# Eleven instead of five dense products between two groups of chunk-local products

## The chip, the cores and the metric

The kernel runs on one core of a Trainium2 chip. The metric is the device time of one execution in microseconds. The engines of the core are TensorE (PE, with its weight loads as PEld), VectorE (DVE), ScalarE (ACT), GpSimd (POOL) and SyncE (SP), which issues most loads. Each works through its own queue in order, and semaphores hold an instruction until what it needs is done.

## What is computed

One encoder block on 512 tokens of width 2048, in float32: a recurrent branch and an attention branch share one normalised input; each is gated and projected, and the two are merged, projected and normalised.

```python
h = rms_norm(x, norm_g)
proj = jnp.einsum('btd,de->bte', h, w_in)             # 2048 -> 86 strips of 128
shifted = centred_shift(proj[..., :SHIFT_WIDTH], shift_mu)
...
def _wkv_step(S, inp):                                # 512 steps, 16 heads of 64, both directions
    w, kk, b, k, v, r = inp
    sa = jnp.einsum('dbhvk,dbhk->dbhv', S, -kk)
    S = S * w[..., None, :] + sa[..., None] * b[..., None, :] + v[..., :, None] * k[..., None, :]
    o = jnp.einsum('dbhvk,dbhk->dbhv', S, r)
    return S, o
...
o_r = rwkv7_bidir(...) * jax.nn.silu(z_r)
o_a = axial_gqa(q, k, v, q_norm_g, k_norm_g) * jax.nn.silu(z_a)     # 16 heads, 4 key heads
p_r = jnp.einsum('btc,cd->btd', o_r, w_branch_rwkv)
p_a = jnp.einsum('btc,cd->btd', o_a, w_branch_attn)
merged = jax.nn.sigmoid(g_r) * p_r + jax.nn.sigmoid(g_a) * p_a
return rms_norm(x + jnp.einsum('btd,de->bte', merged, w_out), final_norm_g)
```

## The kernel before, in words

**Dense products.** Activations stand transposed, 16 tiles of 128 features by 512 tokens, each split into a high part `hh` and a low part `hl` (float32r). A strip is 128 output features; its weights come in quarters of four 128x128 blocks: SP loads `raw`, ScalarE casts it to `wh` (line 264), VectorE subtracts to get `wl` (line 265; in the attention stage every other quarter on GpSimd). Three products a block (line 291) accumulate a strip in `acc`, a PSUM tile of 128x512 of which there are two. Twelve products make a quarter. All dense products that the program weaves are on line 291: 84 whole strips and two early ones of the input projection, then 16 strips `share_r` on `oq` (the recurrent branch's output) and 16 strips `share_a` on `oah`, `oal` (the output of attention); 4932 in all.

**Weaving.** `Weave.run` writes TensorE's order out. Everything that is not a dense product is a task, a generator that issues some instructions and then yields three numbers: the time in ns that TensorE is thought to need for what was issued (`cost`), the time to wait before the task goes on (`wait`), and a flag that it needs. While no task is due, one dense product after another is issued, each counted as 217 ns. So a `wait` of 1000 puts five dense products behind a step. Dense products are a fixed stock: what is issued at one place is missing at a later one. In the recurrent stage TensorE's order is exactly this one. From the attention stage on, the tile framework's scheduler reorders it somewhat, and it sets the order of the other engines' queues throughout.

**Stages.** First the input's normalisation and transposition. Then the recurrent stage: eight tiles of two heads, both directions, 512 tokens in eight chunks of 64. For tile i `stage_a(i)` prepares the decays, `tile_task(i)` computes, `stage_e(i)` normalises the result (reductions on lines 722 to 730, transpositions `pg` on line 736, gating on lines 742 and 743). Meanwhile the strips of the input projection run; those that are only needed later are stored by ScalarE's queue (line 476). Then the attention stage: 64 units, each scores (`sc`, lines 882 and 883), a maximum, an exponential (line 888), a scaling on GpSimd (line 891), transpositions (`pT`, line 899), a split into `ph` and `pl`, and for each two units the output product (`po`, line 914); beside them the rest of the input projection, then `share_r`, whose gates GpSimd loads (`tgm`, line 956). Then `share_a`, then the output projection.

**The place of the change.** `tile_task` begins with the products inside the chunks (`lr`, line 571), in four groups of two chunks. A group is eight products into two PSUM tiles `lr[0]` and `lr[1]`, taken in turn; in the trace each is two records, so a group is 16. PSUM tiles of this kind (`g_tile`) number three. ScalarE copies a part out (lines 573 and 576), VectorE multiplies the rest with masks (lines 574, 575, 577, 578). Behind the last group come `pv`, `tb` and `pcf`, then 230 dense products while VectorE inverts small blocks, then `pq`, `px` and the serial chain over the chunks (`pa`, `pu`, `px2`). The yield that is changed stands at the end of each of the four groups:

```python
        ac.copy(LB[hi_, :, two, :], lr[1][hi_, :, :, C:128])
        ve.tensor_tensor(out=AL[lo_, :, two, 1, :], in0=lr[1][lo_], in1=m2(lo_, 1, 0, 128), op=ALU.mult)
        ve.tensor_tensor(out=L2[hi_, :, two, 1, 0:C], in0=lr[1][hi_, :, :, 0:C], in1=m2(hi_, 1, 0, C), op=ALU.mult)
        yield 1720, 1000, None
```

Of the kernel before, what the change touches and what calls it, by code (L numbers as in the profile page):

```python
# [224 lines left out]
def emit_all(nc, tc, A, out, dbg):  # L225
# [194 lines left out]
    def g_tile(nm):  # L420
        return pr_.tile([128, T], F32, tag="g", name=nm, bufs=3)
# [124 lines left out]
    def tile_task(i):  # L546
# [16 lines left out]
        for c in range(0, NC, 2):  # L563
            two = slice(c, c + 2)

            lr = [g_tile("lr").rearrange("p (d c t) -> p d c t", d=2, c=2) for _ in range(2)]
            for d in range(2):
                for j in range(2):
                    for eo in range(2):
                        h0 = 64 * eo  # L570
                        pe.matmul(lr[eo][:, d, j, :], lhsT=BK[h0:h0 + 64, d, c + j, :], rhs=AL[h0:h0 + 64, d, c + j, eo, :], start=True, stop=True)  # L571
            m2 = lambda rows, eo, c0_, c1_: mk[rows, :, eo, c0_:c1_].unsqueeze(2).to_broadcast([64, 2, 2, c1_ - c0_])
            ac.copy(LB[lo_, :, two, :], lr[0][lo_, :, :, 0:C])
            ve.tensor_tensor(out=AL[hi_, :, two, 0, :], in0=lr[0][hi_], in1=m2(hi_, 0, 0, 128), op=ALU.mult)
            ve.tensor_tensor(out=L2[lo_, :, two, 0, C:128], in0=lr[0][lo_, :, :, C:128], in1=m2(lo_, 0, C, 128), op=ALU.mult)
            ac.copy(LB[hi_, :, two, :], lr[1][hi_, :, :, C:128])
            ve.tensor_tensor(out=AL[lo_, :, two, 1, :], in0=lr[1][lo_], in1=m2(lo_, 1, 0, 128), op=ALU.mult)
            ve.tensor_tensor(out=L2[hi_, :, two, 1, 0:C], in0=lr[1][hi_, :, :, 0:C], in1=m2(hi_, 1, 0, C), op=ALU.mult)
            yield 1720, 1000, None
        pv = g_tile("pv")  # L580
        for j in range(4):
            pe.transpose(pv[:, j * 128:(j + 1) * 128], v[:, j * 128:(j + 1) * 128], ident)
# [172 lines left out]
    for i in range(NT):  # L755
        W.add(3, stage_a(i))
        W.add(0, tile_task(i))
# [334 lines left out]
```

## Time and profile before

| what | value |
|---|---|
| median of three runs | 1799.01 us (1795.56 to 1801.14) |
| the profiled execution | 1803.82 us, of which the span of the trace is 1801.7 us |
| TensorE, matmuls | 1724.6 us busy, 96% |
| VectorE | 1215.6 us, 67% |
| ScalarE | 814.0 us, 45% |
| GpSimd | 564.4 us, 31% |
| chain that ended last | PE 42%, DVE 3%, all others 1% or less |

The span is one execution as the hardware profiler recorded it. Matmuls are pipelined, and the ends of their records are modelled, so "busy" is the time in which some matmul was under way, and not a measure of how well it ran. The granted clock is the share of TensorE's full speed that the chip granted in a stretch: 1.00 is 2.4 GHz, 0.50 is 1.2 GHz.

### The profile page before, as it was taken

What the parts mean: (1) busy time and instruction counts of PE and PEld (TensorE: products, weight loads), DVE (VectorE), ACT (ScalarE), POOL (GpSimd) and SP (SyncE); (2) the same over time, 40 slices, a digit from 0 to 9 for tenths busy, and PEclk for the clock granted to TensorE, in tenths of its full rate; (3) what the DMA queues carried; (4) which work ended last, traced back from release to release, by engine and by line L of the source; (5) the groups of instructions that cost most, each with busy time, mean ns of one, the idle gap of its engine ahead of it and who ended that gap; (6) DMA issues with size and microseconds to landing.
All of it is one profiled execution on the core that took longest, in us unless ns stands there. A gap on an engine that the chain in (4) does not pass through costs nothing. (4 is left out here: it accounts for less than half of the span.)

```text
span 1801.7 us, 26028 instructions
## 1 busy us (share of the span) xinstructions
PE 1724.6 (96%) x8972; PEld 1440.6 (80%) x8972; DVE 1215.6 (67%) x2354; ACT 814.0 (45%) x1827; POOL 564.4 (31%) x830
## 2 busy tenths in 40 slices
PE   7999999998999998999998999999999999999997
PEld 6877887887887886887887887888788888888876
DVE  6577849759849949858859949543868876443342
ACT  5544444444444444354354453444567665332231
POOL 3131242152152233053152241033546553331110
PEclk9999999999999999999999999999999999999999
DMA  6564323323323322423323323325424332435452
GB/s 219 172 198 118 84 69 103 96 59 101 101 60 101 96 66 86 114 65 96 103 65 104 96 71 94 106 77 161 120 83 137 110 94 80 151 113 152 131 164 111
DMA packets 96851, 194.87 MB, mean 108 GB/s; under 512 B 11088, under 2 KB 11344, under 8 KB 95312
## 3 DMA queue, kind: packets, MB, share of 16 engines
q1 hardware_dynamic: 77616, 152.18, 29.5%
q10 hardware_dynamic: 15264, 28.46, 4.4%
q0 software_dynamic: 3840, 12.59, 2.3%
q8 instruction: 71, 1.16, 0.3%
q14 instruction: 60, 0.49, 0.1%
HBM read 162.77 MB, written 30.41 MB: 107 GB/s over the span
## 5 line engine op out<-in xcount | busy, mean ns | idle before, releaser
L291 PE MATMUL acc<-hh,wl 128*128 128x512 f32 (+1 forms) x1388 | 554.0, 399 | 5.3 <-DVE wl L265 5.2
L291 PE MATMUL acc<-hh,wh 128*128 128x512 f32 (+1 forms) x1388 | 556.5, 401 | 0.6 <-ACT wh L264 0.2
L291 PE MATMUL acc<-hl,wh 128*128 128x512 f32 (+1 forms) x1388 | 555.1, 400 | 1.6 <-DVE hl L386 1.2
L264 ACT CAST wh<-raw 128x512 fp32r<-128x512 f32 x472 | 292.3, 620 | 507.4 <-PE acc L291 347.6
L265 DVE TENSOR_TENSOR wl<-raw,wh 128x512 fp32r<-128x512 f32 x439 | 327.4, 748 | 284.4 <-ACT wh L264 275.8
L291 PEld LDWEIGHTS acc<-hh,wl 128*128 128x128 f32 x1388 | 264.3, 190 | 57.4 <-DVE wl L265 8.5
L291 PEld LDWEIGHTS acc<-hl,wh 128*128 128x128 f32 x1388 | 265.1, 191 | 51.9 <-DVE hl L386 3.1
L291 PEld LDWEIGHTS acc<-hh,wh 128*128 128x128 f32 x1388 | 265.2, 191 | 51.3 <-ACT wh L264 1.4
L673 POOL TENSOR_SCALAR SV<-VT 64x128 f32<-64x128 f32 x256 | 81.2, 317 | 208.3 <-PE px L700 116.5
L706 DVE SCALAR_TENSOR_TENSOR SV<-px,PC,sd 64x64 f32<-64x64 f32 x224 | 63.5, 283 | 81.2 <-PE px L700 75.3
L689 POOL TENSOR_SCALAR sd<-SV,PC 64x64 f32<-64x64 f32 x224 | 89.5, 400 | 17.4
L608 DVE TENSOR_TENSOR B<-B,tm 128x30 f32<-128x30 f32 (+14 forms) x240 | 82.2, 342 | 6.0
L607 DVE TENSOR_TENSOR tm<-B 128x30 f32<-128x30 f32 (+14 forms) x240 | 82.2, 343 | 5.8
L291 PE MATMUL acc<-oq,wh 128*128 128x512 f32 x256 | 83.4, 396 | 1.9 <-ACT oq L946 1.9
L1023 PE MATMUL of<-wl,mh 128*128 128x512 f32 x192 | 75.1, 391 | 2.2 <-DVE wl L265 2.2
L527 POOL TENSOR_TENSOR ks<-ks,k 128x512 f32<-128x512 f32 x8 | 15.8, 1969 | 192.0 <-ACT wh L264 111.7
L571 PE MATMUL lr<-AL,BK 64*128 64x128 f32 x512 | 49.9, 314 | 26.6 <-DVE s L728 13.7
L678 PEld LDWEIGHTS pa<-SV,AL 128*128 128x128 f32 x512 | 68.0, 193 | 8.7 <-POOL SV L673 2.3
L1024 PE MATMUL of<-wh,ml 128*128 128x512 f32 x192 | 74.7, 389 | 0.0
L700 PEld LDWEIGHTS px<-SV,L 128*128 128x128 f32 x512 | 68.6, 195 | 7.3 <-ACT SV L694 1.7
L571 PEld LDWEIGHTS lr<-AL,BK 64*128 64x128 f32 x512 | 41.2, 212 | 41.6 <-issue 14.2
L678 PE MATMUL pa<-SV,AL 128*128 128x64 f32 x512 | 67.3, 273 | 2.5 <-DVE SV L706 2.5
(688 smaller groups left out, 2938.8 us busy)
## 6 DMA issues: line engine op xcount, KB each, us to landing
raw<-in_w_in_dram SPq DMA_DIRECT2D x344, 256.0 KB, 3.1
raw<-in_wo_dram SPq DMA_DIRECT2D x64, 256.0 KB, 2.8
fsp<-tg ACTq DMA_DIRECT2D x60, 256.0 KB, 2.5
tsp<-la ACTq DMA_DIRECT2D x32, 256.0 KB, 3.6
la<-tsp SPq DMA_DIRECT2D x8, 1024.0 KB, 5.5
raw<-in_wbr_dram SPq DMA_DIRECT2D x32, 256.0 KB, 2.9
tgm<-fsp POOLq DMA_DIRECT2D x32, 256.0 KB, 3.6
raw<-in_wba_dram SPq DMA_DIRECT2D x32, 256.0 KB, 2.9
```

The costliest lines, as they stand in the source:

```text
L264: ac.copy(dst_hi, src)
L265: (eng or ve).tensor_tensor(out=dst_lo, in0=src, in1=f(dst_hi), op=ALU.subtract)
L291: pe.matmul(acc[:, tok], lhsT=w[1 if u == 2 else 0][:, j, :], rhs=(xl if u == 1 else xh)[:, kt, tok], start=(kt == 0 and u == 0 and tok.st ...
L571: pe.matmul(lr[eo][:, d, j, :], lhsT=BK[h0:h0 + 64, d, c + j, :], rhs=AL[h0:h0 + 64, d, c + j, eo, :], start=True, stop=True)
L607: se.tensor_tensor(out=tv, in0=B[:, 0:s, s:s + 1].to_broadcast([128, s, n]), in1=B[:, s:s + 1, s + 1:32].to_broadcast([128, s, n]), op=ALU ...
L608: se.tensor_tensor(out=B[:, 0:s, s + 1:32], in0=B[:, 0:s, s + 1:32], in1=tv, op=ALU.add)
L673: po.tensor_scalar(out=SV[v0:v0 + 64, d, eo], in0=src.unsqueeze(1).to_broadcast([64, 2, C]), scalar1=1.0, scalar2=0.0, op0=ALU.mult, op1=A ...
L678: pe.matmul(pa[:, d, eo, :], lhsT=AL[:, d, cc[d], eo, :], rhs=SV[:, d, eo, 0, :], start=True, stop=True)
L689: po.tensor_scalar(out=sd[h, d, eo, :], in0=SV[h, d, eo, 0, :], scalar1=PC[h, d, cc[d]:cc[d] + 1], scalar2=0.0, op0=ALU.mult, op1=ALU.add)
L700: pe.matmul(px2[:, d, eo, :], lhsT=L2[:, d, cc[d], eo, :], rhs=SV[:, d, eo, 1, :], start=True, stop=True)
L1023: pe.matmul(acc, lhsT=mh[:, dt, tok(tt)], rhs=w[1], start=False, stop=False)
L1024: pe.matmul(acc, lhsT=ml[:, dt, tok(tt)], rhs=w[0], start=False, stop=(dt == NKT - 1))
```

## The change

Two numbers of one yield: the time counted for a group falls from 1720 to 900 ns, the wait behind it rises from 1000 to 2300 ns. In the count of 217 ns a product that is eleven dense products instead of five. Nothing is computed otherwise.

```diff
--- before.py
+++ after.py
@@ -576,7 +576,7 @@
             ac.copy(LB[hi_, :, two, :], lr[1][hi_, :, :, C:128])
             ve.tensor_tensor(out=AL[lo_, :, two, 1, :], in0=lr[1][lo_], in1=m2(lo_, 1, 0, 128), op=ALU.mult)
             ve.tensor_tensor(out=L2[hi_, :, two, 1, 0:C], in0=lr[1][hi_, :, :, 0:C], in1=m2(hi_, 1, 0, C), op=ALU.mult)
-            yield 1720, 1000, None
+            yield 900, 2300, None
         pv = g_tile("pv")
         for j in range(4):
             pe.transpose(pv[:, j * 128:(j + 1) * 128], v[:, j * 128:(j + 1) * 128], ident)
```

What the planner makes of it is seen in the order of TensorE's queue. Below is what stands in tile 2 from the third group on, before (an `acc` row is one dense product, the `lr` row a whole group, `pg` belongs to the previous tile):

```order
L571 MATMUL lr<-AL,BK 128x128 x8
L291 MATMUL acc<-hh,wl 128x512
L291 MATMUL acc<-hh,wh 128x512
L291 MATMUL acc<-hl,wh 128x512
L291 MATMUL acc<-hh,wl 128x512
L291 MATMUL acc<-hh,wh 128x512
L571 MATMUL lr<-AL,BK 128x128 x8
L736 MATMUL pg<-con,ow 64x128 x8
L291 MATMUL acc<-hl,wh 128x512
L582 MATMUL pv<-con,v 128x128 x4
L633 MATMUL tb<-con,BK 128x128 x4
```

And now, from the same third group:

```order
L571 MATMUL lr<-AL,BK 128x128 x8
L291 MATMUL acc<-hh,wl 128x512
L291 MATMUL acc<-hh,wh 128x512
L291 MATMUL acc<-hl,wh 128x512
L291 MATMUL acc<-hh,wl 128x512
L291 MATMUL acc<-hh,wh 128x512
L291 MATMUL acc<-hl,wh 128x512
L291 MATMUL acc<-hh,wl 128x512
L736 MATMUL pg<-con,ow 64x128 x8
L571 MATMUL lr<-AL,BK 128x128 x8
L291 MATMUL acc<-hh,wh 128x512
L291 MATMUL acc<-hl,wh 128x512
```

Behind the third group there are seven dense products, then `pg`, then the fourth group; eleven dense products, of which two are shown, follow before `pv`. The first two gaps have eleven dense products each instead of five. A tile takes 426 dense products instead of 402 (in the first tile the third gap has eleven, too).

Since a strip is 48 products, the strips now end at other places of a tile, and ScalarE's queue changes with them. Before, its rows in tile 1 around the copies from `pq` (line 649) and from `px` (line 657) are these; line 476 is the store of a gate strip, whose data VectorE writes:

```order
L264 CAST wh<-raw 128x512
L473 ACTIVATE tg<-acc 128x512
L649 COPY LQ<-pq 32x8x32 x4
L476 DMA fsp<-tg 128x512
L657 COPY XP<-px 32x8x32 x4
L680 COPY a0s<-pa 64x128
```

Now:

```order
L649 COPY LQ<-pq 32x8x32 x4
L530 ACTIVATE e_2099<-cs_2093 128x512
L532 ACTIVATE la<-la 128x512
L531 ACTIVATE cs_2093<-cs_2093 128x512
L657 COPY XP<-px 32x8x32 x4
L680 COPY a0s<-pa 64x128
```

The store and its activation have gone from this place, and three exponentials of the next tile's decays (lines 530 to 532) stand there.

The dense products that the recurrent stage now takes are missing at the end of the attention stage. Before, TensorE's rows around the last output product `po` were these; `oq` rows belong to `share_r`, `oah` and `oal` rows to `share_a`:

```order
L291 MATMUL acc<-oq,wh 128x512 x2
L291 MATMUL acc<-oq,wl 128x512
L914 MATMUL po<-ph,VS 128x256 x4
L914 MATMUL po<-pl,VS 128x256 x4
L291 MATMUL acc<-oq,wh 128x512 x2
L291 MATMUL acc<-oq,wl 128x512
L291 MATMUL acc<-oah,wh 128x512
L291 MATMUL acc<-oal,wh 128x512
L291 MATMUL acc<-oah,wl 128x512
L291 MATMUL acc<-oah,wh 128x512
```

Now the last twelve rows up to the last `po` hold no dense product:

```order
L882 MATMUL sc<-KH,Q 128x512
L883 MATMUL sc<-KL,Q 128x512
L899 MATMUL pT<-con,pr 128x128 x4
L914 MATMUL po<-ph,VS 128x256 x4
L899 MATMUL pT<-con,pr 128x128 x4
L914 MATMUL po<-pl,VS 128x256 x4
L899 MATMUL pT<-con,pr 128x128 x4
L914 MATMUL po<-ph,VS 128x256 x4
L899 MATMUL pT<-con,pr 128x128 x4
L914 MATMUL po<-pl,VS 128x256 x4
L914 MATMUL po<-ph,VS 128x256 x4
L914 MATMUL po<-pl,VS 128x256 x4
```

Behind it stand six products of the first two `share_a` strips, which need the last head's output, and then the third strip. From the scores of unit 55 (counted from 1) to the last `po` there are twelve dense products, all of `share_a`.

## Rows read from the trace of the kernel before

**Rows 1.** the page, busy us (share of the span) and instructions of the engines

```profile
PE 1724.6 (96%) x8972; PEld 1440.6 (80%) x8972; DVE 1215.6 (67%) x2354; ACT 814.0 (45%) x1827; POOL 564.4 (31%) x830
```

**Rows 2.** who waited for it: us in total, times, longest us; TensorE

```profile
PE lr L571 <- DVE s L728: 13.7, 3, 5.0
PE lr L571 <- DVE L L575: 12.9, 6, 3.4
```

**Rows 3.** timeline of TensorE at `lr`: start us, us, tile, count [idle before <-releaser]

```profile
149.98 1.13 PE L571 MATMUL lr<-AL,BK 64*128 64x128 f32 x14 [1.60 <-DVE L L575]
...
557.83 1.18 PE L571 MATMUL lr<-AL,BK 64*128 64x128 f32 x14 [3.25 <-DVE L L575]
...
696.40 1.83 PE L571 MATMUL lr<-AL,BK 64*128 64x128 f32 x13 [5.04 <-DVE s L728]
...
1092.82 1.13 PE L571 MATMUL lr<-AL,BK 64*128 64x128 f32 x14 [0.56 <-DVE L L575]
```

**Rows 4.** timeline of TensorE, then VectorE, tile 2

```profile
278.63 1.16 PE L571 MATMUL lr<-AL,BK 64*128 64x128 f32 x16
...
283.02 0.69 DVE L727 TENSOR_REDUCE s<-os__2533 128x8 f32<-128x512 f32 x1 [0.70 <-ACT os__2533 L726]
283.74 0.69 DVE L574 TENSOR_TENSOR AL<-lr,con 64x512 f32<-64x512 f32 x1
284.45 0.41 DVE L575 TENSOR_TENSOR L<-lr,con 64x256 f32<-64x256 f32 x1
```

**Rows 5.** stretches: busy us (records) PE, PEld, DVE, ACT, POOL; granted clock; DMA

```profile
149.20:152.60 3.40, 2.62 (x20) 2.03 (x22) 2.88 (x7) 0.73 (x2) 0.00 (x0) 1.00 0.33 116
227.70:234.50 6.80, 6.25 (x21) 5.48 (x22) 1.97 (x6) 2.30 (x9) 1.25 (x5) 0.50 0.14 39
285.70:289.10 3.40, 3.40 (x14) 2.23 (x13) 3.26 (x8) 1.39 (x4) 2.03 (x1) 0.50 0.47 125
558.80:562.20 3.40, 3.40 (x15) 2.32 (x15) 3.31 (x7) 0.73 (x2) 2.03 (x1) 0.50 0.32 76
961.50:968.30 6.80, 4.72 (x21) 3.59 (x23) 5.93 (x13) 3.76 (x8) 1.86 (x2) 0.50 0.16 39
1600.00:1650.00 50.00, 50.00 (x220) 41.04 (x219) 16.62 (x25) 13.29 (x22) 6.68 (x5) 1.00 0.44 129
```

**Rows 6.** timeline of TensorE, ScalarE and TensorE at `pu`, tiles 1 and 5

```profile
228.25 1.11 PE L693 MATMUL pu<-a0s,XP 128*128 128x64 f32 x4 [3.61 <-ACT a0s L681]
...
226.16 1.49 ACT L657 COPY XP<-px 32x256 f32<-32x256 f32 x4 [5.54 <-DVE tg L475]
...
774.95 0.66 PE L693 MATMUL pu<-a0s,XP 128*128 128x64 f32 x4 [0.24 <-ACT a0s L681]
```

**Rows 7.** timeline of one attention unit: TensorE, ScalarE, GpSimd, VectorE

```profile
1486.04 0.40 PE L883 MATMUL sc<-KL,Q 128*128 128x512 f32 x1
...
1487.68 0.79 ACT L888 ACTIVATE pr<-sc,st__14072,qs 128x512 f32<-128x512 f32 x1
...
1488.95 0.70 POOL L891 TENSOR_SCALAR pr<-pr,st__14072 128x512 f32<-128x512 f32 x1 [0.83 <-DVE st__14072 L889]
...
1489.14 0.69 DVE L265 TENSOR_TENSOR pl<-pT,ph 128x512 fp32r<-128x512 f32 x1 [0.39 <-ACT ph L264]
```

**Rows 8.** timeline of ScalarE and GpSimd behind the last head; its DMAs to landing

```profile
1524.91 0.58 ACT L918 COPY ov<-po 64x512 f32<-64x512 f32 x1 [2.59 <-PE po L914]
1527.67 0.62 ACT L264 CAST oah<-oa 128x512 fp32r<-128x512 f32 x1 [1.66 <-POOL oa L922]
...
1529.55 1.65 POOL L956 DMA_DIRECT2D tgm<-fsp  x3 [1.92 <-DVE oal L265]
...
tgm<-fsp POOLq DMA_DIRECT2D x3, 256.0 KB, 4.1
```

**Rows 9.** timeline of GpSimd and VectorE, a scaling beside a subtraction

```profile
1505.72 1.65 POOL L891 TENSOR_SCALAR pr<-pr,st__14283 128x512 f32<-128x512 f32 x1
...
1505.38 0.90 DVE L265 TENSOR_TENSOR wl<-raw,wh 128x512 fp32r<-128x512 f32 x1 [0.35 <-ACT wh L264]
```


## The prediction

> **What bounds the kernel now.** I read the busy shares first: TensorE is busy 96% of the span, the next engine 67% [rows 1]. A span can then only shorten where TensorE stands still or runs at half its clock, so the second view is TensorE's waits. The largest entry is the chunk-local product `lr`: 13.7 + 12.9 = 26.6 us in nine waits [rows 2]. The third view, the timeline at these waits, shows where they sit: always at the second of a tile's four groups, after two of its 16 records, when the product into the second `lr` tile needs a PSUM buffer that the first group still holds. Tile 1 waits 1.60 us, six tiles wait 3.25 to 5.04 us, the last one twice about 0.6 us [rows 3]. The reader is to see the releaser: VectorE. Its queue brings the previous tile's normalisation ahead of the first group's evacuation: in tile 2 the group starts on TensorE at 278.63, but VectorE first does a reduction for the normalisation at 283.02, for which it even waits 0.70 us for ScalarE, and the evacuation that frees the buffer ends only at 284.86 [rows 4]. VectorE is late here for a reason that lies ahead of the group, so TensorE's own order doesn't move that moment.
>
> The fourth view is the granted clock. Behind the wait in tile 2 it is 0.50 of full speed (1.2 instead of 2.4 GHz) for 3.4 us, behind that in tile 7 for 6.8 us; behind the 1.60 us wait it stays at 1.00 [rows 5]. Over the six long waits it is three times 3.4 and three times 6.8 us, 30.7 us, which cost half of that, 15.4 us.
>
> **The change, part by part.** No instruction is added: 4932 dense products on line 291 before and after. They move: six more go into the first two gaps of each tile, the third takes seven and the `pg` transpositions instead of five, and eleven instead of one stand behind the last group. That is 24 a tile, 192 in all, taken from the end of the attention stage. Each twelve bring one weight load on SP's queue, one cast on ScalarE and one subtraction on VectorE (0.69 us) along. VectorE has room for it: a group's evacuation is 2 x (0.69 + 0.41) = 2.2 us [rows 4]; between groups TensorE now has 1.2 us of `lr` and 11 x 0.227 = 2.5 us of dense products (220 in 50 us [rows 5]), 3.7 us against 2.2 + 0.69 = 2.9. Before it was 2.3 against about 2.5: VectorE set that pace.
>
> (a) Waits at `lr`. Six dense products more are 1.36 us of work between group one and the blocked product, and VectorE's moment stays. Tile 1 goes from 1.60 to 0.24, the six long ones lose 1.36 each (8.2), the last tile's 1.2 goes. In tile 4, whose wait is the shortest of the six, VectorE's new queue has the evacuation ahead of that reduction, 0.70 + 0.69 = 1.4 us earlier [rows 4]. Sum 12.2 us. Bounds: nothing if VectorE slips as far as TensorE, all 26.6.
>
> (b) Half clock behind them. The waits left are about 2.1, 3.0, 0.5, 3.7, 2.1 and 3.0 us. Behind the shortest of the long waits, 3.25 us, the clock fell (the stretch from 558.8) [rows 5], behind 1.60 us it didn't; most of the waits left lie between these. I count four of six still followed by half clock, for 4.3 us on average (three short stretches, one long): 17.2 us, 8.6 lost instead of 15.4. Gain 6.8, bounds 0 and 15.4.
>
> (c) A wait that isn't at `lr`. In tile 1 the product `pu` waited 3.61 us, because ScalarE's queue held the store of a gate strip, which waited 5.54 us for VectorE, between two copies [rows 6]; behind it lie 6.8 us at half clock [rows 5]. The strips now end elsewhere, and in ScalarE's new order that store isn't there. Tile 5 had that order before and waited 0.24 us [rows 6]. Gain 3.4 + 3.4, taken as 6 (0 to 6.8). The same store in tile 4 keeps its place, and so its wait.
>
> (d) The end of attention. This is what the change costs. The dense products that cover attention run out 192 earlier: from unit 55 of 64 on, TensorE's new order holds twelve of them, none behind the scores of the last unit, and then none that can run until the last head is finished. From the rows, one unit needs 3.2 us from the end of its scores (1486.44) to the end of its scaling (1489.65), then come a transposition (some 0.4), a cast (0.62 [rows 8]) and a subtraction (0.69): about 5.2 us with the handovers to its output product [rows 7]. TensorE's work in a unit I estimate by columns: two products of 512, four of 256, four transpositions of 128 taken as 1.5 of 512, so 5.5 x 0.227 = 1.25 us. ScalarE has an exponential (0.79) and a cast, some 1.6 us with handovers. For the last pair of units this chain is bare: 5.2 less 2.1 us of older work, 3 us. For the eight units before, in flight two by two, I put six handovers of 0.5 us: together 6 us (3 to 15). Behind the last output product the head is finished: its copy started at 1524.91, its cast ended at 1528.29, 3.4 us later; the gate load of the next products is issued at 1529.55 and lands 4.1 us later [rows 8], and the merge (0.69 us) must free an accumulator before the third strip of products can start: 9.4 us after the copy's start. In these TensorE has six products, 1.4 us. That is 8.0 us idle, where before dense products ran. The recurrent branch's output projection (products on `oq`), which starts early in the attention stage, meets an emptier pipeline: 1.5 us more (0 to 4). Half clock behind the two waits at the end: 1.7 us (0 to 3.4). Sum 17.2 us, bounds 11 and 30.
>
> The price of the scaling in this chain is itself open. On GpSimd it takes 0.70 us, but 1.65 us where VectorE subtracts beside it (`wl`, `oal`), which then takes 0.90 instead of 0.69 [rows 7, 9]. I take 0.70 since in the bare stretch VectorE's new order has two subtractions of two SBUF tensors, not one a unit; with 1.65 throughout, some 1 us for each of the last pairs, the loss in (d) is 4 us larger, and the range holds that. The Trainium skill ("SBUF — State Buffer", section on its two separate sides) says that VectorE and GpSimd lock a shared port pair for a whole instruction when VectorE reads two SBUF inputs; by that rule a subtraction from PSUM doesn't block the scaling, and the sum stays at 17.2; without it, 21.
>
> Sum: -12.2 - 6.8 - 6 + 17.2 = -7.8 us. The profiled execution took 1803.8 us (span 1801.7, 2.1 us around it), 4.8 above the median of the runs, 1799.0. I apply the difference to both: 1796.0 for a like execution, **1791.2 us** for the median, 0.4% faster. About 0.3% (5.4 us) is what this measurement can tell from no change.
>
> **The rivals.** *The end of attention outweighs it* (slower). The ten bare units run strictly in pairs, since `sc` has two buffers: five pairs at 5.2 + 0.9 = 6.1 us are 30.5 us against 10 x 1.25 + 12 x 0.227 = 15.2 us of TensorE work, 15 us idle, and the sparse work drops the clock for half of it, +4; with 8.0 + 1.7 behind and 2 at `oq` that is 31. Against the gain of 25 this gives +6, 1805 us. It decides from a loss of 30 us on. For it: the bare chain of the rows; against it: four `pr` buffers and two outputs in flight let pairs overlap, and ScalarE needs only 1.6 us a unit. Chance 0.20.
>
> *The wait moves instead of going* (no change). VectorE's new order has the previous tile's last two gate operations, which wait for `pg`'s copy and a load, ahead of the fourth group's evacuation; if that keeps `tb` or the fourth group waiting 1 us in seven tiles, the gain is 18, and the net about zero, 1799 us. The same time comes out where the clock drops behind the shorter waits as often as before. For it: `pg` already has a wait per tile. Chance 0.25.
>
> *The cover isn't missed* (much faster). If the bare units overlap fully and the gate load comes early, the end costs 6 us and the net is -19, 1780 us. Against it: the in-order queue on GpSimd puts that load behind the last head. Chance 0.10.
>
> **How the numbers follow.** The forecast holds 0.45 (1782 to 1794), so faster is 0.45 + 0.10 = 0.55, same 0.25, slower 0.20. The range reaches from the far rival's 1780, less 2 us for the spread of runs, to 1807, 2 above the slow one; beyond it I leave some 0.15.
>
> **What would show it.** Right: `lr` waits of about 14 us instead of 26.6, still at the second group; half-clock stretches behind four tiles; no 3.6 us wait at `pu` in tile 1; TensorE idle for 6 us inside the last units of attention and 8 us behind them, with the gate load as last releaser. Wrong: waits at `pg`, `tb` or the fourth group of over 1 us a tile; the long waits unchanged, which would mean that VectorE follows TensorE; idle time of 20 us or more at the end of attention; or a clock that doesn't fall at all.

## The result, and the profile after

The changed kernel takes **1791.69 us** (median of 7 runs, 1787.47 to 1795.63), the kernel before 1802.51 us in the same session (7 runs, 1795.56 to 1805.54): a ratio of 0.9946, with a 95% interval of 0.9932 to 0.996. Forecast were 1791.2 us and a ratio of 0.9957; the change is 10.8 us, where 7.8 were forecast. Its profiled execution took 1792.16 us (span 1789.9), 11.7 us less than that of before.

The page's busy line shows TensorE's share unchanged; answers to [rows 1]:

```profile
PE 1717.1 (96%) x8972; PEld 1431.3 (80%) x8972; DVE 1221.1 (68%) x2360; ACT 812.6 (45%) x1827; POOL 554.0 (31%) x824
```

TensorE's waits of the changed kernel (us in total, times, longest), against [rows 2]:

```profile
PE lr L571 <- DVE s L728: 9.6, 3, 3.7
PE pu L693 <- ACT a0s L681: 5.8, 10, 3.1
...
PE lr L571 <- DVE L L575: 4.4, 3, 2.1
PE acc L291 <- ACT oq L946: 4.0, 1, 4.0
PE tb L633 <- ACT VT L584: 3.6, 5, 0.7
PE acc L291 <- ACT oah L264: 3.4, 1, 3.4
...
PE acc L291 <- DVE tgm L988: 2.3, 1, 2.3
...
PE lr L571 <- ACT wh L264: 1.4, 1, 1.4
```

`lr`, with gaps too short for this view, comes to 16.3 us instead of 26.6. The `pg` waits (seven of 0.87 us before) are gone, `tb` has 4.4 instead of 1.1 us. Three entries at the bottom of the attention stage are new or longer: `oq` 4.0 (1.9 before), `oah` and `tgm`.

The timeline of TensorE at `pu` of tile 1 and at the second `lr` group of tile 2 (start, duration, in brackets the idle time before and its releaser), against [rows 3] and [rows 6]:

```profile
228.72 0.66 PE L693 MATMUL pu<-a0s,XP 128*128 128x64 f32 x4 [0.24 <-ACT a0s L681]
283.94 1.13 PE L571 MATMUL lr<-AL,BK 64*128 64x128 f32 x14 [2.09 <-DVE L L575]
```

At the same place tiles 3, 4 and 5 wait 2.97, 1.42 and 3.67 us, tiles 6 and 7 wait 2.09 and 2.98 us. Every wait but that of tile 4 is what was forecast, to 0.1 us.

The windows of the changed kernel (the first number behind the stretch is its length, then come the busy time and the records of PE, PEld, DVE, ACT and POOL, the granted clock, and the DMA's share and GB/s): one behind a wait at `lr` that stays at full speed, three that don't, the start of the `oq` products, the first us behind the last head, the last ten units of attention, everything behind their last output product, and then the two stages (from the first `lr` to the first scores, and from there to the last dense product). They answer to [rows 5]:

```profile
283.90:290.70 6.80, 6.76 (x50) 5.43 (x51) 6.50 (x13) 3.84 (x9) 2.17 (x2) 1.00 0.22 56
423.00:426.40 3.40, 3.40 (x9) 2.71 (x10) 3.28 (x6) 0.47 (x2) 0.43 (x1) 0.53 0.28 77
696.10:702.90 6.80, 5.89 (x24) 4.88 (x25) 5.37 (x11) 1.39 (x5) 1.66 (x1) 0.52 0.33 97
969.10:972.60 3.50, 3.50 (x13) 2.75 (x12) 3.41 (x7) 0.85 (x3) 0.88 (x1) 0.54 0.49 132
1320.70:1327.50 6.80, 4.58 (x11) 3.55 (x12) 4.60 (x7) 4.70 (x10) 2.44 (x4) 0.52 0.85 321
1518.70:1528.90 10.20, 7.93 (x19) 5.66 (x18) 5.19 (x7) 3.09 (x5) 5.29 (x7) 0.51 0.56 175
1489.85:1514.18 24.33, 22.57 (x142) 18.19 (x140) 20.84 (x53) 17.56 (x38) 11.44 (x14) 1.00 0.03 11
1514.18:1603.90 89.72, 84.07 (x342) 66.64 (x343) 40.21 (x61) 27.22 (x46) 34.23 (x32) 0.94 0.41 126
145.80:1293.90 1148.10, 1118.18 (x6084) 937.98 (x6083) 845.14 (x1675) 508.85 (x1249) 342.58 (x610) 0.99 0.34 95
1293.90:1603.90 310.00, 295.55 (x1515) 245.05 (x1514) 220.88 (x446) 169.16 (x336) 152.52 (x160) 0.97 0.34 104
```

And of the kernel before, everything behind the last output product:

```profile
1524.87:1615.10 90.23, 90.23 (x387) 72.54 (x386) 43.77 (x65) 28.74 (x49) 35.01 (x32) 1.00 0.43 135
```

Behind the shortest long waits (2.09 us) the clock stays at 1.00; behind 2.97, 3.67 and 2.98 us it is at half for 3.4, 6.8 and 3.4 us. The recurrent stage holds 23.9 us at half clock, where the profile of before has 58.0.

In the last ten units TensorE counts as busy for 22.57 of 24.33 us. That is not a measure of what is lost there: the ends of its records are modelled, so a record that waits a little for its turn still looks covered. The starts tell more. The stretch holds 20 products for scores, 52 transpositions, 56 output products and 12 dense products; in the kernel before these follow one another every 0.23, 0.11, 0.117 and 0.227 us, so they are 19.7 us of work. Some 4.7 us are lost, against 0.2 us in the same ten units of before. Behind the last output product the 341 dense products (a window counts a record at its border, too) need 12.2 us more than at 0.227 us each, the 385 of before 2.7 us more. So some 4.5 us of the end's price lie in the last ten units and 9.5 us behind them.

Behind the last output product (timeline; the wait of 3.39 us is for the cast of the last head, and the second one is released by the merge that the late gate load holds up), against [rows 8]:

```profile
1517.56 0.73 PE L291 MATMUL acc<-oah,wh 128*128 128x512 f32 x2 [3.39 <-ACT oah L264]
1518.77 1.69 POOL L956 DMA_DIRECT2D tgm<-fsp  x3 [1.91 <-PE acc L291]
1521.78 1.40 DVE L988 SCALAR_TENSOR_TENSOR tgm<-tgm,acc 128x512 f32<-128x512 f32 x2 [0.57 <-DMA tgm<-fsp]
1522.53 0.80 PE L291 MATMUL acc<-oah,wh 128*128 128x512 f32 x1 [2.27 <-DVE tgm L988]
```

### The profile page after: what moved, and what is told of

It reads as the page before. It is cut to its first block, busy times and chain, and to the rows that moved or that the text cites. A ratio compares the mean times of both kernels' runs of the same rounds, so it can differ in the third digit from the quotient of the medians.

```text
span 1789.9 us, 26075 instructions
## 1 busy us (share of the span) xinstructions
PE 1717.1 (96%) x8972; PEld 1431.3 (80%) x8972; DVE 1221.1 (68%) x2360; ACT 812.6 (45%) x1827; POOL 554.0 (31%) x824
## 5 line engine op out<-in xcount | busy, mean ns | idle before, releaser
L265 DVE TENSOR_TENSOR wl<-raw,wh 128x512 fp32r<-128x512 f32 x445 | 331.9, 748 | 278.7 <-ACT wh L264 268.3
L527 POOL TENSOR_TENSOR ks<-ks,k 128x512 f32<-128x512 f32 x8 | 15.2, 1901 | 223.4 <-ACT wh L264 84.0
L678 PEld LDWEIGHTS pa<-SV,AL 128*128 128x128 f32 x512 | 67.3, 191 | 10.2 <-POOL SV L673 2.3
L1022 PE MATMUL of<-wh,mh 128*128 128x512 f32 x192 | 66.1, 389 | 0.0
L700 PE MATMUL px<-SV,L 128*128 128x64 f32 x512 | 65.6, 271 | 0.0
```

The source lines that it names most:

```text
L265: (eng or ve).tensor_tensor(out=dst_lo, in0=src, in1=f(dst_hi), op=ALU.subtract)
L678: pe.matmul(pa[:, d, eo, :], lhsT=AL[:, d, cc[d], eo, :], rhs=SV[:, d, eo, 0, :], start=True, stop=True)
L700: pe.matmul(px2[:, d, eo, :], lhsT=L2[:, d, cc[d], eo, :], rhs=SV[:, d, eo, 1, :], start=True, stop=True)
L1022: pe.matmul(acc, lhsT=mh[:, dt, tok(tt)], rhs=w[0], start=(dt == 0), stop=False)
```

## The experiments

Twelve runs were made: ten other kernels, and both kernels once more. For all of them the same two stretches were read from the windows view: the recurrent stage (first `lr` to first scores) and the rest up to the last dense product; idle is the length less TensorE's busy time (with modelled ends, so it shows the long waits and not all lost time), half clock the time at a granted clock of about 0.5, all in us. "Moved" is how many dense products stand ahead of the first scores beyond the kernel before's 3914. The gain is 1133.4 us plus 0.227 us for each product moved, less the stage's length; the price of the rest is its length plus 0.227 us for each product moved, less 336.3 us. (The expectation of the fifth kernel used 0.217 us, the planner's count, and 48 and 144 products instead of the 54 and 150 that moved in the first two kernels, and so has smaller prices.)

| kernel | ratio (95%) | moved | recurrent: length, idle, half clock | gain | rest: length, idle, half clock | price |
|---|---|---|---|---|---|---|
| before | 1 | 0 | 1133.4, 44.5, 58.0 | 0 | 336.3, 4.9, 3.4 | 0 |
| before, again | one run | 0 | 1129.5, 45.4, 47.8 | 3.9 | 336.4, 4.9, 3.4 | 0.1 |
| changed | 0.9946 (0.9932 to 0.996) | 192 | 1148.1, 29.9, 23.9 | 28.9 | 310.0, 14.4, 17.1 | 17.3 |
| changed, again | one run | 192 | 1148.3, 28.7, 27.3 | 28.7 | 310.2, 14.8, 17.1 | 17.5 |
| first gap only | 0.9988 (0.9977 to 0.9999) | 54 | 1133.1, 36.9, 47.8 | 12.6 | 332.7, 9.6, 13.7 | 8.7 |
| later gaps only | 0.9964 (0.9951 to 0.9977) | 150 | 1149.5, 36.1, 47.8 | 18.0 | 314.4, 12.5, 6.8 | 12.2 |
| long wait only | 1.0033 (1.002 to 1.0046) | 192 | 1170.2, 42.8, 51.2 | 6.8 | 307.2, 14.4, 6.8 | 14.5 |
| refund in every tile | 0.9991 (0.9977 to 1.0004) | 6 | 1131.9, 41.8, 51.2 | 2.9 | 332.0, 3.1, 0 | -2.9 |
| refund in the last tile | 0.9952 (0.9935 to 0.997) | 144 | 1136.3, 28.9, 23.9 | 29.8 | 321.2, 13.5, 17.1 | 17.6 |
| `pg` later | 0.9986 (0.9974 to 0.9998) | 21 | 1135.8, 44.5, 58.0 | 2.4 | 330.6, 5.0, 0 | -0.9 |
| shifted to the first gap | 0.9964 (0.995 to 0.9977) | 192 | 1149.6, 30.2, 23.9 | 27.4 | 307.1, 14.5, 6.8 | 14.4 |
| first gap of 20 | 0.9946 (0.9928 to 0.9964) | 200 | 1150.3, 28.2, 20.5 | 28.5 | 306.1, 13.7, 3.4 | 15.2 |
| no normalisation | 0.9975 (0.9964 to 0.9987) | 0 | 1129.7, 41.2, 54.6 | 3.7 | 335.1, 5.0, 0 | -1.2 |
| square on GpSimd | 0.9919 (0.9898 to 0.994) | 192 | 1146.2, 25.8, 27.3 | 30.8 | 309.6, 15.1, 13.7 | 16.9 |

Two executions of the kernel before differ by 3.9 us in the recurrent stage, so a gain within 4 us of another says nothing by itself.

### Only the first gap, only the later gaps

```diff
-            yield 1720, 1000, None
+            yield (900, 2300, None) if c == 0 else (1720, 1000, None)
```

> Only the first gap of each tile gets eleven products, the other gaps keep five: 48 products move instead of 192. Theory (the gain lies at the second group, where the queue of VectorE is late, and the price lies in the cover at the end of attention): the waits at lr go from 26.6 to about 16 us as in the changed kernel, with a half-clock gain behind them of some 8 us; the last units of attention keep their products between them (40 stand between the last scores and the last output product, 45 in the kernel before behind it, here none), so only the 6 us behind the last head are lost. About 12 us faster than the kernel before, 1790 us, ratio 0.993. Rival (all gaps must grow, because VectorE paces every group): the lr waits appear at the third and fourth group instead, gain at lr under 5 us, ratio 0.998 or more.

```diff
-            yield 1720, 1000, None
+            yield (1720, 1000, None) if c == 0 else (900, 2300, None)
```

> The reverse: the first gap keeps five products, the other gaps get eleven, so 144 products move. Theory: the waits at lr at the second group stay at 25 to 27 us with their half clock, the end of attention loses about what the changed kernel loses there (some 14 us: all cover behind the last scores is gone), so 5 to 15 us slower than the kernel before, ratio 1.003 to 1.008. Rival (the later gaps bring the gain): ratio 0.996 or less, lr waits under 18 us.

TensorE's waits of the first kernel:

```profile
PE lr L571 <- DVE L L575: 13.0, 8, 3.0
PE pu L693 <- ACT a0s L681: 7.6, 7, 3.4
PE pg L736 <- ACT gc L738: 7.2, 7, 2.0
...
PE px L653 <- ACT LQ L649: 2.3, 2, 1.2
```

and of the second:

```profile
PE lr L571 <- DVE L L575: 15.0, 5, 4.4
PE lr L571 <- DVE s L728: 13.0, 3, 4.3
```

With the first gap alone, `lr` falls to 16.0 us (13.0 and 3.0), as forecast. But the kernel gains little: the end costs 8.7 us for 54 products, and new waits appear at `px`, where ScalarE's copies from `pq` now stand behind exponentials (two of 1.17 us, each with 6.8 us at half clock). With the later gaps alone, `lr` waits as long as ever (28.0 us), and yet the kernel is faster; the theory had it slower. Gone are the `pg` waits (6.1 us), 4.8 us at `pu` and some half clock. So the theory was right on where `lr` waits and wrong that the gain lies there alone. The two gains, 12.6 and 18.0, add up to 30.6 us against the 28.9 of both; the prices, 8.7 and 12.2, to more than the 17.3 of both (each alone uncovers the last head already).

### The same price without the cover, and the cover given back

```diff
-OPT = dict(..., subwait=50000, ...)
+OPT = dict(..., subwait=55208, ...)
```

> The kernel before with five products in every gap, but the long wait of each tile (while VectorE inverts) counted 5.2 us longer, so that 24 more products a tile stand there: the same 192 products are missing at the end of attention, none of them stands where a wait was. Theory: lr waits stay at 26.6 us, and the end of attention alone costs what the changed kernel paid there, 14 to 17 us with its half clock: ratio 1.007 to 1.010. Rival (the cover at the end isn't missed; what the changed kernel lost there has another cause): ratio 0.999 to 1.003.

```diff
-            yield 1720, 1000, None
+            yield 900, 2300, None
...
-OPT = dict(..., subwait=50000, ...)
+OPT = dict(..., subwait=44792, ...)
```

> The changed kernel with the long wait of each tile counted 5.2 us shorter, so 24 products a tile fewer stand there and the end of attention gets its 192 back (3920 instead of 4106 products stand ahead of the first scores, as against 3914 before). VectorE's inverse had 10 to 13 us to spare there, so nothing new should wait. Theory: the gain at lr and pu is kept and the loss of 14 to 17 us at the end is returned: about 1776 us, ratio 0.985 (0.982 to 0.988). Rival (the 24 products fewer make VectorE late at the next products, or the end's loss doesn't come from the cover): ratio 0.993 or more.

Taking 192 products from the end for no use costs 14.5 us there, and the kernel is slower by 0.33%; less than expected, because the recurrent stage gains 6.8 us though no product was put where a wait was. `pu` happened to wait 4.6 instead of 8.2 us with the strips ending elsewhere, and 6.8 us less stand at half clock. The end's price is shown, and also that a gain of this size can come from where the strips end.

Giving the products back did return it (no idle time behind the last head), but the recurrent stage lost it all again. Two of TensorE's waits, and the timeline of tile 4's chain on TensorE and VectorE:

```profile
PE pa L678 <- DVE SV L706: 17.1, 9, 4.4
PE lr L571 <- DVE L L575: 12.4, 6, 2.7
```

```profile
640.84 1.73 DVE L541 SCALAR_TENSOR_TENSOR ks<-r,par,ks 128x512 f32<-128x512 f32 x1 [2.47 <-POOL ks L540]
642.50 1.75 DVE L265 TENSOR_TENSOR wl<-raw,wh 128x512 fp32r<-128x512 f32 x1
644.16 1.22 DVE L706 SCALAR_TENSOR_TENSOR SV<-px,PC,sd 64x64 f32<-64x64 f32 x4
644.58 1.73 PE L678 MATMUL pa<-SV,AL 128*128 128x64 f32 x7 [4.36 <-DVE SV L706]
```

The chain now starts 24 products earlier, and the next tile's preparation (line 541, which itself waits for GpSimd) stands in VectorE's queue ahead of the state update. The inverse did have its slack; what I hadn't looked at was the queue behind it.

### Giving back in the last tile only

```diff
-        yield 432, OPT['subwait'], None
+        yield 432, OPT['subwait'] - (10416 if i == NT - 1 else 0), None
```

> The changed kernel, with the long wait of the last tile alone counted 10.4 us shorter: 48 products (144 instead of 192 moved) go back to the end of attention, at the one place where no next tile's preparation shares VectorE's queue and the inverse had 14 us to spare. What the first four kernels showed of the end of attention (from the first scores to the first product of the output projection, against the products left for it) is 6.7 us lost at 54 products moved, 9.4 at 150, 15.3 and 12.6 at 192. Theory now (the price isn't in proportion: the first strip missing uncovers the last head, the rest only thins the units): nothing new waits in the recurrent stage, and 3 to 6 us come back: ratio 0.992 to 0.994 against the kernel before's 1, about 1787 us. Rival (the price is in proportion, a quarter of it comes back, and shorter waits upset VectorE's queue as in the kernel with the refund in every tile, where pa waited 17 us): 0.995 or more.

Nothing new waits in the recurrent stage (gain 29.8), but the price stays: 17.6 us at 144 products moved, where the later gaps alone pay 12.2 at 150. The windows of line 291 alone tell where the 48 products went; first the changed kernel, then this one, each from the first scores to those of unit 55:

```profile
1293.90:1489.80 195.90, 122.04 (x473) 88.26 (x472) 0.98 0.34 105
```

```profile
1279.93:1483.40 203.47, 133.69 (x521) 97.38 (x520) 0.98 0.35 108
```

All 48 stand ahead of unit 55. From there on 12 dense products stand in the last ten units and 341 behind the last output product, the same as in the changed kernel, so the end is as bare as there. Counted by starts, 1.6 us come back ahead of unit 55 and 2.0 us more are lost in the last units. The kernel with the later gaps alone keeps 33 products in the last units and loses 2.7 us less behind them, with 3.4 instead of 10.2 us at half clock there. The ratio, 0.9952, can't be told from the changed kernel's.

### `pg` later

```diff
-OPT = dict(..., gn=15000, ...)
+OPT = dict(..., gn=20000, ...)
```

> The kernel before with one number changed: the normalised result's transpositions pg are due 20 instead of 15 us after the normalisation, which puts them between the tb transpositions instead of right behind the fourth lr group. No products are put between the lr groups, some 20 fewer stand behind the first scores. Theory: the pg wait of 0.87 us in seven tiles (6.1 us) is a wait for the PSUM buffers that the fourth lr group still holds, and goes; lr waits stay at 26 us; the net is 4 to 6 us, ratio 0.997. Rival (the wait belongs to the number of buffers, and moves to tb or elsewhere): same time, ratio 0.999 to 1.001.

The `pg` wait is gone, as a wait for the fourth group's buffers should be, but `lr` rose from 26.6 to 32.4 us, so that the idle time of the stage is unchanged at 44.5. The rival holds in kind: removed alone, this wait only moves (the ratio, 0.9986, lies just below the rival's 0.999 to 1.001). It goes for good where the later gaps grow.

### Shifting the same products to the first gap, and lengthening it

```diff
-            yield 900, 2300, None
+            yield 900, (4300, 1000, 2300, 1650)[c // 2], None
```

> The changed kernel with the same 24 products more a tile, but 20 instead of 11 of them in the first gap, 5 in the second, 11 in the third, 8 instead of 11 around the fourth. Nothing more is taken from the end of attention. Theory (VectorE's moment of evacuation is set by the previous tile's normalisation, not by TensorE): nine products more in the first gap are 2.04 us, so the waits of 2.09, 2.97, 1.42, 3.67, 2.09 and 2.98 us shrink to 0.05, 0.9, 0, 1.6, 0.05 and 0.9; lr in all 3.5 to 4 instead of 16 us, most of the 13.6 us at half clock behind them goes: 15 us faster than the changed kernel, 1777 us, ratio 0.986. Rival (VectorE follows TensorE, since the loads and subtractions of nine more products stand in its queue): lr waits of 10 us or more, ratio 0.993 or more. A second rival: lr goes but the fewer products behind the second and fourth group bring waits there (third group, pg, tb) of 6 us or more: ratio 0.990.

```diff
-OPT = dict(..., subwait=50000, fwait=6000, gn=15000, ...)
+OPT = dict(..., subwait=48047, fwait=6000, gn=16953, ...)
...
-            yield 900, 2300, None
+            yield 900, (4300 if c == 0 else 2300), None
```

> The changed kernel with nine products more in the first gap of each tile (20, then 11, 11 and 11), these nine taken from the long wait of the same tile while VectorE inverts, and pg kept at its place, seven products behind the third group. The end of attention gets the same products as in the changed kernel. Theory (VectorE owes a fixed amount of work from the previous tile's normalisation to the tb transpositions, and TensorE must have that much of its own between them; shifting products from later gaps only moved the wait): with 20 in the first gap and 11 in each later one the backlog is covered; lr and tb together go from 20.7 us to 4 to 6 us, the 13.6 us of half clock behind lr to 3 to 7, net 15 to 20 us faster than the changed kernel: 1775 us, ratio 0.983 to 0.987. Rival (the nine products bring VectorE nine twelfths of a quarter's subtraction and less slack behind, so that the wait comes back at tb or in the chain, at pa): ratio 0.991 or more.

TensorE in tile 3 of the shifted kernel (second group, third group, first `tb`):

```profile
421.99 1.13 PE L571 MATMUL lr<-AL,BK 64*128 64x128 f32 x14 [0.95 <-DVE s L728]
426.30 2.04 PE L571 MATMUL lr<-AL,BK 64*128 64x128 f32 x14 [1.39 <-DVE L L575]
...
436.88 0.63 PE L633 MATMUL tb<-con,BK 128*128 128x128 f32 x4 [1.64 <-DVE L L575]
```

The second group's wait falls from 2.97 to 0.95 us, by the nine products (in tiles 5 and 7 by 2.0 us, too), as the theory had it: VectorE doesn't follow TensorE. But the rest comes back one group later and at `tb`, as the second rival had it: `lr` and `tb` together are 22.2 us, as against 20.7 in the changed kernel. That suggested that TensorE has to cover VectorE's work from the first group to `tb` as a whole. With 20 products in the first gap and 11 in each later one, `lr` and `tb` fall to 14.4 us, not to the 4 to 6 that this theory gave, and `pa` rises to 9.2 (longest 3.0, line 541 ahead of line 706 again), since the nine products came from the wait ahead of the chain; this rival holds. The gain is 28.5, no different from the changed kernel's, and the ratio is 0.9946 again.

### The normalisation left out

```diff
-        s8 = rw.tile([128, 32], F32, name="s8")
-        ve.tensor_reduce(out=s8[:, 0:8], in_=ow, axis=AX.X, op=ALU.add)
...
-        ve.tensor_tensor(out=ow, in0=ow, in1=s8[:, 24:32].unsqueeze(2).to_broadcast([128, NC, C]), op=ALU.mult)
```

> The kernel before without the normalisation of the recurrent result: the two reductions, three VectorE products, two small ones, ScalarE's square and GpSimd's root of each tile are left out (some 4 us of VectorE a tile), the transpositions pg take the result unnormalised. No products move. Theory (the previous tile's normalisation in VectorE's queue is why the first group is evacuated late): the six waits of 3.2 to 5.0 us at lr fall to about that of the first tile, which has no tile ahead of it, 1.6 us: lr 26 to under 12 us in all, most of the 30 us of half clock behind them goes, 20 to 30 us faster, ratio 0.983 to 0.990. Rival (the evacuation is late for another reason, the decays' preparation or the weights' subtractions in VectorE's queue): lr waits of 20 us or more, ratio 0.996 or more.

Tile 2 in the timeline, in the order of the cause: the decays' sum on VectorE, GpSimd, ScalarE, VectorE's evacuation, TensorE:

```profile
282.12 0.68 DVE L522 TENSOR_TENSOR cs<-cs 128x512 f32<-128x512 f32 x1
282.95 1.26 POOL L523 TENSOR_TENSOR la<-cs,la 128x512 f32<-128x512 f32 x1 [8.05 <-DVE cs L522]
284.25 0.63 ACT L530 ACTIVATE e<-la 128x512 f32<-128x512 f32 x1 [5.72 <-POOL la L523]
284.78 0.35 ACT L573 COPY LB<-lr 64x256 f32<-64x256 f32 x1
285.17 0.69 DVE L574 TENSOR_TENSOR AL<-lr,con 64x512 f32<-64x512 f32 x1 [2.36 <-ACT LB L573]
286.43 1.38 PE L571 MATMUL lr<-AL,BK 64*128 64x128 f32 x14 [3.25 <-DVE L L575]
```

My theory fell. (VectorE loses two reductions, two products, not three, and two small ones: some 3 us a tile.) VectorE is free at 282.80, but the wait is still 3.25 us, and the other five are 3.0 to 4.0; `lr` is 23.2 us in all. VectorE now waits for ScalarE's copy out of the same PSUM buffer, in six tiles 1.9 to 2.6 us, and ScalarE's queue has an exponential of the next tile's decays ahead of that copy. In the kernel before, ScalarE's copy also stood behind something that waits: at 282.36 in tile 2 the square for the normalisation, after 5.46 us of waiting for VectorE. The lateness has two branches, VectorE's queue and ScalarE's, and ScalarE's alone is enough for waits of over 3 us.

The two instructions read different halves of the partitions (line 573 the first 64, line 574 the last 64). The Trainium skill ("PSUM — Partial Sum Buffer", section on PSUM bank collisions) says that two engines may access different quadrants of one bank at the same time. By that rule the chip doesn't ask for this wait; the rows show that it is made all the same, so it comes from the order that the program's semaphores impose. Whether it can be left out was not tried.

### The square on GpSimd, in the changed kernel

```diff
-        ac.activation(os_, ow, AF.Square)
+        po.tensor_tensor(out=os_, in0=ow, in1=ow, op=ALU.mult)
```

> The changed kernel with the square of the normalisation (128x512, a tile one) computed by GpSimd instead of ScalarE; no products move. What the run without the normalisation showed is that VectorE's evacuation (line 574) then waits 1.9 to 2.6 us for ScalarE's copy out of the same buffer (line 573), which stands behind an exponential that waits for GpSimd: the lateness has two branches, VectorE's queue and ScalarE's. With the square gone from ScalarE, its queue has the copy first, and VectorE's has the evacuation ahead of the second reduction (line 727) in every tile, as it was in tile 4 alone. Theory (both branches must be cleared at once): the evacuation ends some 1.4 us earlier in five tiles, lr 16 to 9 us or less, half of the half clock behind it goes (6 us), no new wait: 8 to 12 us faster than the changed kernel, ratio 0.988 to 0.990. Rival (VectorE's whole backlog up to tb decides, as when products were shifted to the first gap, and GpSimd's square of over 1 us delays the decays' preparation): the wait comes back at later groups, at tb or at pa: ratio 0.993 to 0.996.

Tile 2 (evacuation and TensorE's wait), then tile 3 (GpSimd and VectorE's `wl`):

```profile
279.48 0.69 DVE L574 TENSOR_TENSOR AL<-lr,con 64x512 f32<-64x512 f32 x1
280.75 1.13 PE L571 MATMUL lr<-AL,BK 64*128 64x128 f32 x14 [0.72 <-DVE L L575]
...
414.45 1.59 POOL L523 TENSOR_TENSOR la<-cs,la 128x512 f32<-128x512 f32 x1 [8.19 <-DVE cs L522]
414.82 1.76 DVE L265 TENSOR_TENSOR wl<-raw,wh 128x512 fp32r<-128x512 f32 x1
416.00 1.49 POOL L726 TENSOR_TENSOR os__3856<-ow 128x512 f32<-128x512 f32 x1
```

The fastest of all: 1785.73 us (1781.66 to 1790.07), ratio 0.9919. Both branches are shorter, and the waits of tiles 2 and 6 fall from 2.09 to 0.7 us, the 1.4 us that the theory gave. In tiles 3, 5 and 7 they fall by 0.6 only (to 2.35, 3.08, 2.36): there a subtraction `wl`, which takes 0.69 us alone, takes 1.76 beside GpSimd's line 523, in the queue just ahead of the evacuation. It took 1.77 in the changed kernel's tile 3 as well, and hid the wait for the square; so only the reduction that stood behind it (0.67 us) is saved. `lr` is 12.4 us, between the theory's 9 and the changed kernel's 16.3, the half clock is not less (27.3 us), and the ratio lies between the theory's 0.988 to 0.990 and the rival's 0.993 to 0.996. Against the kernel before it is faster without doubt. Against the changed one the profile shows 2 us in the recurrent stage and the ratios differ by 0.0027, some 4.9 us, but the two intervals overlap at their ends (0.9898 to 0.994, 0.9932 to 0.996).

### Both kernels once more

> The kernel before once more, for a second profile of it. Theory: the waits repeat to 0.1 us each; the half-clock stretches behind waits of 3 us or more repeat in place, while some others come or go (one of 10.2 us in the first profile has no wait ahead of it). Rival (the stretches belong to the program): all repeat, the 10.2 us one too.

> The changed kernel once more, for a second profile. Theory: the waits repeat to 0.1 us; the half clock of the recurrent stage comes to 20 to 35 us (23.9 in the first profile), so that its difference to the kernel before (58.0 and 47.8 us in two profiles) is the change's and not the execution's. Rival: 40 us or more, and the clock's share of the gain was chance.

The windows of the kernel before, first profile and second, at two places of the program (stretch behind tile 2's `pq`, where no wait stands ahead; behind the wait of 4.32 us at `lr` in tile 3):

```profile
357.40:367.60 10.20, 10.20 (x40) 9.23 (x39) 8.43 (x8) 5.91 (x17) 5.48 (x4) 0.50 0.10 27
422.20:425.70 3.50, 3.46 (x18) 2.98 (x19) 2.72 (x6) 0.97 (x3) 1.66 (x1) 0.51 0.11 37
```

```profile
353.30:363.50 10.20, 9.15 (x66) 8.16 (x67) 7.37 (x9) 6.48 (x18) 6.68 (x5) 1.00 0.19 53
418.60:425.40 6.80, 6.21 (x36) 4.96 (x36) 5.05 (x11) 1.71 (x4) 1.66 (x1) 0.52 0.12 32
```

The waits repeat to 0.1 us at nearly all places. Tile 1's `lr` waits 1.60 and 0.77 us, and tile 2's chain tells why such a difference is no gain: `pu` and `pa` wait 1.04 and 0.65 us there only where the stretch ahead runs at full clock, since a TensorE at half clock arrives too late to wait. (The two profiles of the changed kernel show the same: 1.05 and 0.64 us there, and neither wait behind 3.4 us at half clock.) The half clock doesn't repeat: 10.2 us without a wait come and go, and behind the same wait it is 3.4 us in one execution and 6.8 in the other. The changed kernel's second profile has 27.3 us in the recurrent stage, so over the four profiles the difference to before is 20 to 34 us of half clock, by half some 10 to 17 us of time, and goes with the change.

## Why the prediction was right

The direction and the mechanism were right, and the ratio to 0.0011. That the time agrees to 0.5 us is luck: the kernel before was measured 3.5 us higher in that session than the 1799.0 us that the forecast started from, and the change is 10.8 us, not 7.8. The difference lies in the recurrent stage, which by lengths gained 28.9 us where (a) to (c) gave 25.0: 14.6 us are less idle time, and 14.3 us go with 34.1 us less at half clock, so half of such a stretch is somewhat too high a price for it.

**(a) Waits at `lr`: right, a little too large.** 10.3 us instead of 12.2. Tile 4 is the miss, 1.42 instead of 0.5: VectorE's queue had the product of a gate strip there (line 475, 0.69 us at 553.08) ahead of the evacuation, and ScalarE's copies, behind the store of that strip, ended at 554.98, when VectorE was just coming free (555.04). The step "VectorE's moment stays" is shown by the nine products more that took 2.0 us off the long waits. The reason given for it, the previous tile's normalisation in VectorE's queue, is only half of it: without the normalisation the waits stay, for ScalarE's queue is late as well. And in tiles 3, 5 and 7, which wait longest, VectorE's queue of the kernel before has a slow subtraction between the normalisation and the evacuation, which the prediction didn't look at (tile 3; in tiles 2, 4 and 6 it stands further ahead in the queue and takes 0.66 or 0.67 us):

```profile
418.58 1.76 DVE L265 TENSOR_TENSOR wl<-raw,wh 128x512 fp32r<-128x512 f32 x1
```

**(b) Half clock behind them: mechanism right, size 1.8 us off.** 13.6 us instead of 30.7, so 8.6 gained, not 6.8: three of six waits are still followed by it, not four. What the forecast didn't have is the half clock at other places than `lr` and tile 1's `pu`: 10.3 instead of 20.5 us; but 10.2 of these 20.5 have no wait ahead and are missing in the second profile of before, too. It also left out the `pg` waits: 6.1 us gone, 3.3 of them back at `tb`.

**(c) `pu` of tile 1: right.** 0.24 us instead of 3.61, as said, and the 6.8 us at half clock behind it are gone.

**(d) The end of attention: the sum right, its parts within 2 us.** The price is 17.3 us by lengths, 17.2 were forecast. Counted by starts, the last ten units lose 4.5 us more than before instead of 6, everything behind the last output product 9.5 us, where 8.0 idle and 1.7 for the clock were forecast, and the rest, 3.3 us instead of 1.5, lies ahead of unit 55; of it 2.1 us are the longer wait where the `oq` products start. That the first and the last of these cancel is luck. Two readings in it were off. Behind the last head TensorE is idle for 5.7 us, not 8.0: the cast took 3.4 us as read off, the gate load, issued at 1518.77, had landed by 1521.78 (3.0 us instead of 4.1), and the six products took 2.7 us at half clock instead of 1.4. And the half clock there, 10.2 us, by this count costs the 3.8 us that remain, not 1.7 (in the kernel with the long wait only, with 3.4 us at half clock there, 1.2 us remain). The sign that was named, 6 us of idle time inside the last units, didn't come (24.33 - 22.57 = 1.8 us), since idle time doesn't show what is lost there. The rival in which units run strictly in pairs gave 30.5 us for a stretch that is 24.3 us long; its 15.2 us of work for TensorE left out that transpositions of 13 units and output products of 14 fall into it (19.7 us). The scaling took 0.69 to 0.71 us in eleven of the last twelve units, as was taken.

**The rivals.** The wait that moves is real and small in the changed kernel (`tb`, 3.3 us), and decides where a wait is removed alone (`pg` later) or products are only shifted. The slower outcome is what the long wait alone shows: the price without the gain.

**Left open.** The refund in the last tile returned nothing because its products landed ahead of unit 55; why the program's order puts them there isn't known, and no kernel was tried that keeps the gain and leaves them behind the last output product. Whether the square on GpSimd with more products left for the end is faster still was not tried.

## What to carry to other kernels

Cover counts where the engine that is waited for is late. Shift it within that engine's backlog and part of the wait shifts with it; take it from the next wait and that one grows. Look behind the named releaser for what *its* queue waits for, and on every engine that touches the same buffer; here two queues were late together, and removing one cause alone showed little. The price of missing cover isn't in proportion to it: the first 54 products taken from the end cost 8.7 us here, for 44 of them had stood behind the last output product; all 192 cost 17.3. And where the ends of records are modelled, compare starts with a stretch at full pace, since busy time hides short delays.

## What the hardware showed that I had not expected

The granted clock differs between executions of one program with the same waits: 58.0 and 47.8 us at half clock in the recurrent stage of the kernel before, 23.9 and 27.3 in the changed one. Half of the difference, 5.1 us, is more than the 3.9 us by which the two profiles of before differ in that stage, so one profile isn't enough to price it.

A subtraction of two SBUF tensors on VectorE (`wl`) takes 0.69 us alone and 1.76 us where GpSimd's line 523 was running as it started: it ends 0.54 us after GpSimd does, and GpSimd's square behind it takes 1.49 instead of 1.03 us. The same pair stands in tiles 3, 5 and 7 of the kernel before, 1.76 us each. The Trainium skill ("SBUF — State Buffer", section on the two separate sides) calls the port pair that the two share "an exclusive lock, not a bandwidth split", held for a whole instruction. The trace agrees in the main, in both directions; that the subtraction ends 0.54 us after GpSimd, and not the 0.69 us that a whole one takes, is a little less than the rule gives.
